# A second ConvGLU's up projection as seven products instead of eight, with the convolution's pad and shift bias moved to ScalarE

## The chip, the core and the metric

The kernel runs on one core of a Trainium2 chip. The time is device microseconds of one execution, the median over runs. TensorE is called PE in the profile, VectorE DVE, ScalarE ACT, GpSimd POOL and SyncE SP.

## The reference

Two layers work on 512 latent and 256 context tokens of width 1024. Layer 0 mixes by windowed attention, layer 1 by a gated recurrence (HGRN2). Each ends with a ConvGLU of width 2816; layer 0 does it for all 768 tokens, layer 1 for the 512 latent ones alone:

```python
def dwconv3(u, w, b):
    up = jnp.pad(u, ((0, 0), (1, 1), (0, 0)))
    return up[:, :-2] * w[0] + up[:, 1:-1] * w[1] + up[:, 2:] * w[2] + b

def conv_glu(h, w_up, conv_w, conv_b, w_down):
    gate, val = jnp.split(h @ w_up, 2, axis=-1)
    return (jax.nn.silu(dwconv3(gate, conv_w, conv_b)) * val) @ w_down
...
        hx2 = rms_norm(x, norm2_g[layer]) * (1.0 + sc2) + sh2
        x = x + g2 * conv_glu(hx2, ffn_w_up[layer], ffn_conv_w[layer], ffn_conv_b[layer], ffn_w_down[layer])
```

Everything is fp32 in and out.

## The kernel before

Activations lie with features on the partitions and tokens along the free axis. An fp32 product is made of three TensorE matmuls in a rounded format: each operand is split into a high part (a rounding copy) and a low part (the remainder), and high by high, high by low and low by high are summed in PSUM.

Weights arrive as fp32 by SP's DMA queue into a raw tile `wr` (pool of two buffers, 1 MB each, two DMAs of 512 KB for one feature tile of the up projection, line 95). ScalarE copies a 512-wide piece into `wh` (L117, or L140 in layer 0's ConvGLU) and VectorE subtracts it to make `wl` (L118, or L141). Pairs `wh`, `wl` come in turn from four pools, some eight pairs ahead of TensorE.

A ConvGLU has 22 feature tiles `ft` of 128 gate and 128 value features. In layer 1 (`ROUNDS[1]`) they go in rounds of 8, 7 and 7 tiles: a round makes its tiles' `g` (the up phase), then the first tile of the next round (`ahead`), and then multiplies the round's tiles into the down projection, eight 128-row blocks of output taken in four pairs (the down phase: matmuls `dn`, accumulated into `xl` by VectorE, L1023). In the last round there is no `ahead`; the first pair's products with all tiles but the last are put before the last tile's `g`. Then come the output's transposes `xo`.

The norm's scale and shift: the matmuls run on activations times gain with the shifts as two extra columns (512 and 513), and the per-token scale `R` is applied to the products as they leave PSUM. `R` is made while tile 0 is multiplied: `nss` sums the squares (L524), VectorE makes `rv` (L428), POOL the inverse root `rs` (L429), VectorE a diagonal `dg` (L529), TensorE spreads it (`nR`, L533), ScalarE copies it to `R`.

Layer 0's ConvGLU uses a scheme that makes the four quadrant products of a 2 by 2 block matrix product with seven products instead of eight. `load_pair` makes four weight totals on VectorE (L136, `s` and two pieces in place in `wr`) and seven operand pairs; `gate_pair` runs the seven products (L188, 84 matmuls of half the columns, PSUM tiles `pZ`, `pY`, `pV`), with ScalarE evacuating four of them, VectorE adding three and multiplying two by `R`, and POOL multiplying the value half by `R`. `combos` makes the seven activation combinations. Layer 1 used `load_w` (four pairs) and `gate_plain` (L912): 96 matmuls of 256 or 258 columns, four multiplies by `R` on VectorE. Both then run the same lines: pad `G` (L983), shift bias `cb` (L985), `u` (ScalarE, L987), two fused multiply-adds (L988, L989), silu (L991), the gate product (L992), and g's high and low parts (L995, L996).

In layer 1 `hgrn_out` runs right ahead: it multiplies the recurrence's output into `xl` in pairs of blocks (L895) and prepares the ConvGLU's activations, so far by `shifts` and `scaled` (L362, L363). The order in which engines get their instructions comes from a scheduler with priorities; weight work is moved ahead by a fixed offset (`W_AHEAD`).

Of the kernel before, what the change touches and what calls it, by code (L numbers as in the profile page):

```python
# [34 lines left out]
SH, C0, TW = 512, 514, 770  # L35
# [29 lines left out]
def ap(t, off, *dims):  # L65
    return bass.AP(t.tensor, t.offset + off, [list(t.ap[0])] + [list(d) for d in dims])
# [6 lines left out]
class Kernel:  # L73
# [442 lines left out]

    def row_factor(self, acc, lat_only, tmp, pp, tag, width, R, sh, dg):


        nc = self.nc  # L520
        nt = (LAT if lat_only else TOK) // P
        ps = pp.tile([P, width], F32, tag=tag, name="nss")
        for i in range(nt):
            nc.tensor.matmul(ps[:, 2 * i:2 * i + 2], lhsT=acc[:, i * P:(i + 1) * P], rhs=self.ones[:, 0:2], start=True, stop=True)  # L524
# [4 lines left out]
        nc.vector.tensor_tensor(dg, ap(self.ident[:, 0:1], 0, (0, nt), (1, P)), ap(r[:, 0:1], 0, (1, nt), (0, P)), op=ALU.mult)  # L529
        for t, c in (((0, 0),) if lat_only else ((0, 0), (4, C0))):  # L530
            m = min(4, nt - t)
            pr = pp.tile([P, width], F32, tag=tag, name="nR")
            nc.tensor.matmul(pr[:, 0:m * P], lhsT=self.ones, rhs=dg[:, t:t + m].rearrange("p t c -> p (t c)"), start=True, stop=True)  # L533
            nc.scalar.activation(R[:, c:c + m * P], pr[:, 0:m * P], AF.Copy)
        nc.vector.memset(R[:, SH:C0], sh)
        if R.shape[1] > TW:
            nc.vector.memset(R[:, TW:], sh)

    def spread(self, r, nt, out, tmp, tag="dg"):

# [354 lines left out]
            self.nc.vector.scalar_tensor_tensor(x[:, d], ps[:, lo:hi], self.modc(l, v, which, d), x[:, d], op0=ALU.mult, op1=ALU.add)  # L895


    def gate_plain(self, ft, ops, hn, G, gg, R, rows, half, tmp, bank):


        nc = self.nc
        act = lambda k: (hn[:, 0, k], hn[:, 1, k])
        cols = ((0, 256), (256, C0))
        for j, dst in enumerate((G[:, 1:1 + C0], gg)):
            ps = [bank("pd")[:, 0:hi - lo] for lo, hi in cols]
            for _ in self.mm_steps(ops[j], range(KT), act, [(o, lo) for o, (lo, _) in zip(ps, cols)]):
                pass
            for _ in rows:
                pass

            for o, (lo, hi) in zip(ps, cols):
                nc.vector.tensor_tensor(dst[:, lo:hi], o, R[:, lo:hi], op=ALU.mult)  # L912
# [45 lines left out]
    def ffn(self, l, hs, R, rows, lat_only, tmp, acp, bk, gp, done, side=None):  # L958
        nc, a = self.nc, self.a
        wup, wdn = a["ffn_w_up"][l], a["ffn_w_down"][l]  # L960
        half = C0 // 2 if lat_only else hs[0].shape[3]
        n = LAT if lat_only else TW
        cw = self.cw[l]

# [8 lines left out]
        def up(ft):  # L973

            ws_ = [self.wcols(wup, ft * P, P), self.wcols(wup, DFF + ft * P, P)]
            ops = self.load_w(ws_) if lat_only else self.load_pair(ws_, tmp)
            if side:
                next(side, None)

            G = tmp.tile([P, 2 * half + 2], F32, tag="G", name="G", bufs=gb)  # L980
            gg = tmp.tile([P, 2 * half], F32, tag="ny", name="gg", bufs=2)
            (self.gate_plain if lat_only else self.gate_pair)(ft, ops, hs, G, gg, R, rows, half, tmp, bank)
            nc.vector.tensor_copy(ap(G[:, 0:1], 0, (TW + 1, nv)), G[:, 1 + SH:1 + SH + nv])  # L983
            cb = tmp.tile([P, 2], F32, tag="cb", name="cb")
            nc.vector.tensor_scalar(cb[:, :nv], G[:, 1 + SH:1 + SH + nv], ws[:, ft:ft + 1], cw[:, 66 + ft:67 + ft], op0=ALU.mult, op1=ALU.add)  # L985
            u = tmp.tile([P, n], F32, tag="nt", name="u", bufs=gb)
            nc.scalar.activation(u, G[:, 1:1 + n], AF.Copy, scale=cw[:, 22 + ft:23 + ft])  # L987
            nc.vector.scalar_tensor_tensor(u, G[:, 0:n], cw[:, ft:ft + 1], u, op0=ALU.mult, op1=ALU.add)  # L988
            nc.vector.scalar_tensor_tensor(u, G[:, 2:2 + n], cw[:, 44 + ft:45 + ft], u, op0=ALU.mult, op1=ALU.add)  # L989
            for v, c, m in segs:  # L990
                nc.scalar.activation(u[:, c:c + m], u[:, c:c + m], AF.Silu, bias=cb[:, v:v + 1])  # L991
                nc.vector.scalar_tensor_tensor(gg[:, c:c + m], gg[:, c:c + m], gg[:, SH + v:SH + v + 1], u[:, c:c + m],  # L992
                                               op0=ALU.subtract, op1=ALU.mult)
            g2 = gp.tile([P, 2, n], F32R, tag="g", name="g")
            nc.scalar.activation(g2[:, 0], gg[:, :n], AF.Copy)  # L995
            nc.vector.tensor_tensor(g2[:, 1], gg[:, :n], f(g2[:, 0]), op=ALU.subtract)  # L996
            return g2
# [273 lines left out]
        es.close()  # L1271
        return part

    def hgrn_out(self, part, hn, acc, tmp, pj):
        nc = self.nc
        self.shifts(1, 1, hn)
        wout = self.a["hgrn_w_out"][0]
        oh = part[0]
        act = lambda k: (oh[:, 0, k], oh[:, 1, k])
        for dp in range(KT // 2):  # L1280
            if dp < 2:
                w, ps, ks = part[1][dp], part[2][dp], (KT - 1,)
# [19 lines left out]
    def run(self, stop=99):  # L1302
# [74 lines left out]
        lv = self.pool(e2, "lv", 2, PSUM)  # L1377
        part = self.hgrn(hn2[0], R, accs[0], hb, pj, lv, sc)
        hc = self.pool(rs, "hC", 1, right=True)
        hn = self.hn_tile(hc, "hn3", C0)  # L1380
        ot = self.pool(es, "ot", 1)
        acc = Rp.tile([P, LAT], F32, tag="acc", name="acc2")
        self.hgrn_out(part, hn, acc, ot, pj)
        if stop == 4:
            self.nc.sync.dma_start(out=self.dbg["dbg"][:, :, :, :LAT], in_=f(part[0][:, :, :, :LAT]))
            e2.close(); rs.close(); es.close(); hB.close(); pjs.close(); top.close(); return
        R = Rp.tile([P, C0], F32, tag="R", name="R2")
        e2.close()
        pjs.close()
        es.close()  # L1390
# [62 lines left out]
```

## Time and profile before

| what | value |
|---|---|
| median of 3 runs | 1862.78 us (1858.02 to 1863.27) |
| the profiled execution | 1863.46 us, span 1861.4 us |
| mean granted TensorE clock | 0.991 |
| layer 1: last part of `hgrn_out` to the end of the row sums | 1439.7 to about 1478 us |
| layer 1, round 0: up from 1481.3, down from | 1581.0 us |
| round 1: up from, down from | 1625.2, 1705.7 us |
| round 2: up from, down from, end of span | 1744.2, 1813.3, 1861.4 us |

Times in the profile's rows are microseconds from the start of the span. A row of stretches gives, for each engine, the busy time and the number of instructions in brackets, then the granted clock as a share of full speed. A row of the timeline gives start, duration, engine, line, operation, the output and inputs, the shape, the count, and in square brackets how long the engine was idle before and what ended that. A row of groups gives the count, busy time and mean duration, and after the second bar the idle time before such instructions with what ended most of it. Instructions of one engine overlap by some tenths of a microsecond, so the distance from start to start is less than a duration.

### The profile page before, as it was taken

Reading aid. Unit: us, or ns where it says so; the run is one execution under the profiler, and the core shown is the slowest. Engines: PE = TensorE matmul, PEld = TensorE weight load, DVE = VectorE, ACT = ScalarE, POOL = GpSimd, SP = SyncE. Lnnn points to the kernel's source line nnn. Section 1 sums busy time; section 2 is a strip of 40 time slices with the busy share of each in tenths; the row PEclk is TensorE's granted clock in tenths of the full one; section 3 lists DMA queues with packets and bytes.
Section 4 is the critical chain, followed back from the end, with each engine's and each line's share of the span. In section 5 each row is a group of like instructions: output and inputs, shape, how many; then the busy total and the mean of one; then the engine's idle time right before and its main releaser. Section 6 shows DMA issues by size and latency. Waiting matters only on the chain.

```text
span 1861.4 us, 32314 instructions
## 1 busy us (share of the span) xinstructions
PE 1798.5 (97%) x13326; PEld 1575.2 (85%) x13326; DVE 1214.4 (65%) x2265; ACT 755.0 (41%) x1486; POOL 218.8 (12%) x219
## 2 busy tenths in 40 slices
PE   6999999998999999999999999999998999999998
PEld 4976786687888888888898888888996799899997
DVE  5576667466868686767777676677765666365462
ACT  4355555465534443434445323333332433233332
POOL 1233333103200000100001100111110000000000
PEclk9999999999999999999999999999999999999999
DMA  9204104232333343333313222121220332333321
GB/s 307 70 23 159 46 24 167 71 102 69 124 114 102 113 136 94 111 96 120 117 54 105 58 58 58 35 56 37 58 69 24 90 92 91 94 96 94 91 83 65
DMA packets 204415, 166.42 MB, mean 89 GB/s; under 512 B 5149, under 2 KB 198254, under 8 KB 199150
## 3 DMA queue, kind: packets, MB, share of 16 engines
q1 hardware_dynamic: 196608, 160.47, 28.1%
q10 hardware_dynamic: 7662, 3.92, 0.7%
q8 instruction: 104, 1.70, 0.4%
q14 instruction: 41, 0.34, 0.1%
HBM read 162.27 MB, written 2.10 MB: 88 GB/s over the span
## 4 chain that ended last, share of the span: by engine, by line
PE 88%; DMA 4%; DVE 4%; ACT 1%; issue 1%; POOL 0%; SPq 0%; ACTq 0%; POOLq 0%; DVEq 0%
PE dn L170 15%; PE pd L170 14%; PE pZ L188 8%; PE pf L170 8%; PE pV L188 4%; PE pjq L598 4%; PE pv L170 4%; PE ao L170 4%; PE ho L170 3%; PE pq L170 3%; PE pv L824 3%; PE pt L816 2%; PE ada L309 2%; PE pgate L170 2%; PE kv L598 2%; DMA wr<-in_ffn_w_up 2%
## 5 line engine op out<-in xcount | busy, mean ns | idle before, releaser
L117 ACT ACTIVATE wh<-wr 128x512 fp32r<-128x512 f32 (+2 forms) x328 | 194.5, 608 | 462.4 <-DMA wr<-in_ffn_w_up 76.9
L118 DVE TENSOR_TENSOR wl<-wr,wh 128x512 fp32r<-128x512 f32 (+2 forms) x328 | 220.0, 678 | 137.6 <-ACT wh L117 137.0
L170 PE MATMUL dn<-g,wh 128*128 128x512 f32 (+1 forms) x1056 | 262.9, 357 | 0.0
L170 PE MATMUL pd<-hn,wh 128*128 128x256 f32 (+1 forms) x1408 | 227.6, 284 | 1.9 <-issue 1.9
L170 PEld LDWEIGHTS dn<-g,wh 128*128 128x128 f32 x1056 | 175.2, 189 | 29.7 <-ACT g L995 0.3
L170 PEld LDWEIGHTS pd<-hn,wh 128*128 128x128 f32 x1408 | 194.5, 190 | 3.3 <-issue 3.1
L188 PE MATMUL pZ<-hs,wh 128*128 128x386 f32 x704 | 184.5, 343 | 2.2 <-DVE hs L393 1.1
L170 PE MATMUL dn<-g,wl 128*128 128x512 f32 (+1 forms) x528 | 159.5, 356 | 0.0
L140 ACT ACTIVATE wh<-wr 128x512 fp32r<-128x512 f32 x132 | 82.3, 629 | 160.5 <-DMA wr<-in_ffn_w_up 38.1
L170 PE MATMUL pd<-hn,wl 128*128 128x256 f32 x704 | 141.9, 283 | 0.0
L188 PEld LDWEIGHTS pZ<-hs,wh 128*128 128x128 f32 x704 | 127.8, 190 | 14.3 <-issue 5.9
L141 DVE TENSOR_TENSOR wl<-wr,wh 128x512 fp32r<-128x512 f32 x132 | 95.9, 733 | 47.9 <-ACT wh L140 46.6
L188 PE MATMUL pZ<-hs,wl 128*128 128x386 f32 x352 | 119.2, 341 | 4.4 <-DVE wl L141 4.4
L170 PE MATMUL pf<-hn,wh 128*128 128x512 f32 (+1 forms) x512 | 117.6, 344 | 2.9 <-DVE xc L1023 1.9
L170 PEld LDWEIGHTS pd<-hn,wl 128*128 128x128 f32 x704 | 109.2, 190 | 0.0
L926 POOL TENSOR_TENSOR gg<-gg,R 128x772 f32<-128x772 f32 x22 | 48.9, 2224 | 456.5 <-DVE gg L925 443.6
L1023 DVE SCALAR_TENSOR_TENSOR xl<-dn,mod,xl 128x512 f32<-128x512 f32 x72 | 53.9, 749 | 73.7 <-PE dn L170 73.7
L170 PEld LDWEIGHTS dn<-g,wl 128*128 128x128 f32 x528 | 87.6, 188 | 14.8
L188 PE MATMUL pV<-hs,wh 128*128 128x386 f32 x352 | 92.0, 340 | 5.0 <-ACT hs L392 5.0
L170 PEld LDWEIGHTS pf<-hn,wh 128*128 128x128 f32 x512 | 79.4, 189 | 15.6 <-DVE xc L1023 2.3
L598 PE MATMUL pjq<-wh,hn 128*128 128x256 f32 x384 | 77.8, 290 | 0.0
L188 PEld LDWEIGHTS pZ<-hs,wl 128*128 128x128 f32 x352 | 66.3, 189 | 7.4 <-DVE wl L141 5.7
(298 smaller groups left out, 3787.0 us busy)
## 6 DMA issues: line engine op xcount, KB each, us to landing
wr<-in_ffn_w_up SPq DMA_DIRECT2D x88, 512.0 KB, 5.2
wada<-in_ada_w SPq DMA_DIRECT2D x40, 1024.0 KB, 4.9
wr<-in_hgrn_w_in SPq DMA_DIRECT2D x40, 512.0 KB, 4.2
ar<-in_ada_w SPq DMA_DIRECT2D x32, 256.0 KB, 7.1
wr<-in_ffn_w_down SPq DMA_DIRECT2D x8, 896.0 KB, 4.8
wr<-in_attn_w_in SPq DMA_DIRECT2D x6, 1024.0 KB, 8.2
wr<-in_ffn_w_down SPq DMA_DIRECT2D x12, 384.0 KB, 3.6
wr<-in_attn_w_out SPq DMA_DIRECT2D x8, 512.0 KB, 5.7
```

The source lines that it names most:

```text
L117: nc.scalar.activation(wh, src, AF.Copy)
L118: nc.vector.tensor_tensor(wl, src, f(wh), op=ALU.subtract)
L140: nc.scalar.activation(ops[i][0], src, AF.Copy)
L141: nc.vector.tensor_tensor(ops[i][1], src, f(ops[i][0]), op=ALU.subtract)
L170: nc.tensor.matmul(o, lhsT=wt, rhs=at[:, t0:t0 + o.shape[1]], start=(first and n == 0 and i == 0), stop=(last and n == len(ks) - 1 and i = ...
L188: self.nc.tensor.matmul(ps, lhsT=wt, rhs=at, start=(first and k == 0 and i == 0), stop=(k == nk - 1 and i == 2), skip_group_check=not first)
L309: nc.tensor.matmul(ps[32 * j:32 * j + 32, 0:512], lhsT=self.cs[:, k, :], rhs=raw[:, j * 512:(j + 1) * 512], start=(k == 0), stop=(k == KT ...
L598: nc.tensor.matmul(out, lhsT=x, rhs=y[:, wk], start=(start and k == 0 and j == 0), stop=(stop and k == KT - 1 and j == 2))
L816: nc.tensor.transpose(pt[:, j * P:(j + 1) * P], pr[j][:, b * P:(b + 1) * P], self.ident)
L824: nc.tensor.matmul(pv[a * HD:(a + 1) * HD, 0:256], lhsT=V[:, tl, g, :], rhs=pT[:, a * 256:(a + 1) * 256], start=(b == 0), stop=(b == len(t ...
L926: times = lambda eng, o, x, y: eng.tensor_tensor(o, x, y, op=ALU.mult)
L1023: nc.vector.scalar_tensor_tensor(x[:, d], o, self.modc(l, v, 5, d), x[:, d], op0=ALU.mult, op1=ALU.add)
```

## The change

Layer 1's up projection goes through `load_pair` and `gate_pair` as layer 0's does, on halves of 258 columns (the first 258 tokens; the other 254 with two shift columns and two zero columns): 84 matmuls of 258 columns for a tile. `hgrn_out` makes the seven activation combinations, the first five for each pair of blocks inside its loop and the last two behind it. POOL's multiply of the value half by `R` then runs in layer 1 too. In both layers the pad and the shift bias become ScalarE instructions. `gate_plain` is gone.

```diff
@@ def spread R @@
-        if R.shape[1] > TW:
-            nc.vector.memset(R[:, TW:], sh)
+        n = C0 if lat_only else TW
+        if R.shape[1] > n:
+            nc.vector.memset(R[:, n:], sh)
...
-    def gate_plain(self, ft, ops, hn, G, gg, R, rows, half, tmp, bank):
...
@@ ffn @@
-        half = C0 // 2 if lat_only else hs[0].shape[3]
+        half = hs[0].shape[3]
...
-            ops = self.load_w(ws_) if lat_only else self.load_pair(ws_, tmp)
+            ops = self.load_pair(ws_, tmp)
...
-            (self.gate_plain if lat_only else self.gate_pair)(ft, ops, hs, G, gg, R, rows, half, tmp, bank)
-            nc.vector.tensor_copy(ap(G[:, 0:1], 0, (TW + 1, nv)), G[:, 1 + SH:1 + SH + nv])
+            self.gate_pair(ft, ops, hs, G, gg, R, rows, half, tmp, bank)
+            nc.scalar.activation(ap(G[:, 0:1], 0, (TW + 1, nv)), G[:, 1 + SH:1 + SH + nv], AF.Copy)
             cb = tmp.tile([P, 2], F32, tag="cb", name="cb")
-            nc.vector.tensor_scalar(cb[:, :nv], G[:, 1 + SH:1 + SH + nv], ws[:, ft:ft + 1], cw[:, 66 + ft:67 + ft], op0=ALU.mult, op1=ALU.add)
+            nc.scalar.activation(cb[:, :nv], G[:, 1 + SH:1 + SH + nv], AF.Identity, scale=ws[:, ft:ft + 1], bias=cw[:, 66 + ft:67 + ft])
...
-    def hgrn_out(self, part, hn, acc, tmp, pj):
+    def hgrn_out(self, part, hs, acc, tmp, pj):
         nc = self.nc
-        self.shifts(1, 1, hn)
+        some = []
...
+            some.append(self.combos(self.halves(1, 1, dp, 258, True, tmp, ("y0", "y1"), 4), dp, hs))
+            next(some[-1])
             for d in (dp, dp + 4):
-                self.scaled(1, 1, d, hn, True)
                 self.square_acc(d, acc, True, tmp, "sg", first=(d == 0))
+        for rest in some:
+            for _ in rest:
+                pass
...
-        hn = self.hn_tile(hc, "hn3", C0)
+        hs1 = hc.tile([P, 7, 2, 4, 258], F32R, tag="hs", name="hs3")
+        hs = [hs1[:, i] for i in range(7)]
...
-        R = Rp.tile([P, C0], F32, tag="R", name="R2")
+        R = Rp.tile([P, 516], F32, tag="R", name="R2")
```

In the changed file the lines of the ConvGLU stand lower: the adds of `gate_pair` are L910, its multiplies L911, pad and bias L968 and L970, the fused operations L973, L974 and L977, the low part of g L981, the residual add of `hgrn_out` L896, and `combos` has L393 (`hs`) and L396 (`y`).

The order of instructions moves as follows. First VectorE between the row sums and the diagonal `dg` that `R` waits for. Before:

```order
L363 SCALAR_TENSOR_TENSOR hn_15134<-xl,gs_126,hn_15134 128x512
L515 TENSOR_TENSOR acc_15138<-acc_15138,sq 128x512
L118 TENSOR_TENSOR wl<-wr,wh 128x512 x2
L428 TENSOR_SCALAR rv<-nss 128x4
L529 TENSOR_TENSOR dg<-cst,rs 128x512
L912 TENSOR_TENSOR G<-pd,R_15337 128x256
```

Changed:

```order
L396 TENSOR_TENSOR y<-y 128x258
L428 TENSOR_SCALAR rv<-nss 128x4
L910 TENSOR_TENSOR G<-t,pY 128x258
L136 TENSOR_TENSOR wr<-wr 128x512
L141 TENSOR_TENSOR wl<-wr,wh 128x512
L396 TENSOR_TENSOR y<-y 128x258 x2
L393 TENSOR_TENSOR hs_15134<-y,hs_15134 128x258
L141 TENSOR_TENSOR wl<-wr,wh 128x512 x3
L393 TENSOR_TENSOR hs_15134<-y,hs_15134 128x258 x2
L529 TENSOR_TENSOR dg<-cst,rs 128x512
```

Eleven instructions, of the last combinations and of the weights of tiles 0 and 1, now stand between `rv` and `dg`, where there was none.

Next VectorE in round 0's up phase, before (most of one tile: two pieces of G, pad and bias, the two fused operations, two pieces of the value, and splits between them):

```order
L912 TENSOR_TENSOR G<-pd,R_15337 128x256
L912 TENSOR_TENSOR G<-pd,R_15337 128x258
L118 TENSOR_TENSOR wl<-wr,wh 128x512
L983 COPY G<-G 128x1
L985 TENSOR_SCALAR cb<-G,wsum,par 128x1
L988 SCALAR_TENSOR_TENSOR u<-G,par,u 128x512
L989 SCALAR_TENSOR_TENSOR u<-G,par,u 128x512
L118 TENSOR_TENSOR wl<-wr,wh 128x512
L912 TENSOR_TENSOR gg<-pd,R_15337 128x256
L912 TENSOR_TENSOR gg<-pd,R_15337 128x258
L118 TENSOR_TENSOR wl<-wr,wh 128x512
L992 SCALAR_TENSOR_TENSOR gg<-gg,u 128x512
```

Changed, from the last split that reads tile 2's raw weights to the first totals of tile 4 (`s_15911` is tile 3's total, `s_16060` tile 4's):

```order
L141 TENSOR_TENSOR wl<-wr,wh 128x512
L910 TENSOR_TENSOR gg<-gg,pV 128x258
L973 SCALAR_TENSOR_TENSOR u<-G,par,u 128x512
L974 SCALAR_TENSOR_TENSOR u<-G,par,u 128x512
L141 TENSOR_TENSOR wl<-wr,wh 128x512
L977 SCALAR_TENSOR_TENSOR gg<-gg,u 128x512
L141 TENSOR_TENSOR wl<-wr,wh 128x512
L910 TENSOR_TENSOR gg<-gg,t 128x258
L136 TENSOR_TENSOR s_16060<-wr 128x512
L910 TENSOR_TENSOR G<-t,pY 128x258
L136 TENSOR_TENSOR wr<-s_15911,wr 128x512
```

The first total of tile 4 needs the raw buffer that this split, the first row, releases, and seven instructions stand between the two.

Last TensorE at the end of the last round's up phase. Before, the last value products are followed by 42 down matmuls in a row and then the first transposes:

```order
L170 MATMUL pd<-hn_15134,wh 128x256
L170 MATMUL pd<-hn_15134,wh 128x258
L170 MATMUL pd<-hn_15134,wl 128x256
L170 MATMUL pd<-hn_15134,wl 128x258
L170 MATMUL dn<-g,wh 128x512 x2
L170 MATMUL dn<-g,wl 128x512
```

Changed, the end of the last product and all that is left before the first transposes:

```order
L188 MATMUL pZ<-hs_15134,wh 128x258 x2
L188 MATMUL pZ<-hs_15134,wl 128x258
L170 MATMUL dn<-g,wh 128x512 x3
L170 MATMUL dn<-g,wl 128x512
L170 MATMUL dn<-g,wh 128x512
L170 MATMUL dn<-g,wl 128x512
L1396 MATMUL xo<-cst,xl 128x128 x4
```

The other 36 down matmuls of that pair now stand among and ahead of the last tile's products. SP's queue has the same loads in the same order, and POOL has 22 multiplies `gg<-gg,R` of 128x516 where it had none.

More of the change, by code (lines that the diff above doesn't have):

```diff
@@ L895, in add_gated @@
             self.nc.vector.scalar_tensor_tensor(x[:, d], ps[:, lo:hi], self.modc(l, v, which, d), x[:, d], op0=ALU.mult, op1=ALU.add)
-    def gate_plain(self, ft, ops, hn, G, gg, R, rows, half, tmp, bank):
[L901 to L912, printed above, removed]
     def gate_pair(self, ft, ops, hs, G, gg, R, rows, half, tmp, bank):
@@ L1379, in run @@
         hc = self.pool(rs, "hC", 1, right=True)
-        hn = self.hn_tile(hc, "hn3", C0)
+        hs1 = hc.tile([P, 7, 2, 4, 258], F32R, tag="hs", name="hs3")
+        hs = [hs1[:, i] for i in range(7)]
         ot = self.pool(es, "ot", 1)
         acc = Rp.tile([P, LAT], F32, tag="acc", name="acc2")
-        self.hgrn_out(part, hn, acc, ot, pj)
+        self.hgrn_out(part, hs, acc, ot, pj)
         if stop == 4:
@@ L1409, in done1 @@
                 nc.sync.dma_start(out=a["out"][0, :, (d - 1) * P:(d + 1) * P].rearrange("(t p) c -> p t c", p=P), in_=ost[0])
-        self.ffn(1, hn, R, rows, True, tmp, acp, bk, gp, done1)
+        self.ffn(1, hs, R, rows, True, tmp, acp, bk, gp, done1)
         es.close()
```

## The prediction

> **What bounds the kernel now.** I read the engine line of the page first, then the chain that ended last, then the last 420 us cut into their stages, since the change lies there.
>
> ```profile
> PE 1798.5 (97%) x13326; PEld 1575.2 (85%) x13326; DVE 1214.4 (65%) x2265; ACT 755.0 (41%) x1486; POOL 218.8 (12%) x219
> ...
> PE 88%; DMA 4%; DVE 4%; ACT 1%; issue 1%; POOL 0%; SPq 0%; ACTq 0%; POOLq 0%; DVEq 0%
> ```
>
> ```profile
> core 0: us, PE busy (x) PEld busy (x) DVE busy (x) ACT busy (x) POOL busy (x), PEclk, DMA share, GB/s
> 520.00:600.00 80.00, 79.58 (x455) 71.68 (x454) 58.28 (x104) 30.23 (x55) 5.95 (x3) 1.00 0.37 116
> 1439.70:1471.40 31.70, 28.47 (x108) 21.64 (x108) 23.40 (x38) 17.02 (x30) 0.00 (x0) 0.88 0.36 100
> 1471.40:1481.30 9.90, 7.32 (x58) 7.03 (x59) 4.31 (x10) 2.51 (x4) 1.01 (x1) 0.99 0.38 106
> 1481.30:1581.00 99.70, 99.70 (x819) 99.18 (x818) 59.30 (x119) 39.88 (x61) 0.00 (x0) 0.98 0.29 85
> 1581.00:1625.20 44.20, 44.20 (x194) 36.10 (x193) 17.43 (x27) 10.44 (x18) 0.00 (x0) 1.00 0.33 96
> 1625.20:1705.70 80.50, 80.50 (x673) 80.48 (x672) 47.32 (x95) 30.23 (x48) 0.00 (x0) 1.00 0.30 88
> 1705.70:1744.20 38.50, 38.50 (x170) 31.53 (x169) 17.04 (x27) 9.89 (x17) 0.00 (x0) 1.00 0.37 107
> 1744.20:1813.30 69.10, 69.10 (x578) 69.06 (x577) 40.29 (x81) 25.40 (x41) 0.00 (x0) 1.00 0.29 86
> 1813.30:1861.40 48.10, 42.94 (x202) 34.61 (x200) 12.44 (x20) 9.98 (x18) 0.00 (x0) 0.99 0.19 63
> ```
>
> TensorE bounds the kernel, and layer 1's ConvGLU most plainly: from 1481.3 to 1813.3 it is never idle. Up phases alternate with down phases (99.7/44.2, 80.5/38.5, 69.1/48.1). In an up phase 672 matmuls take 80.5 us, 0.120 us each; in a down phase 168 take 38.5 us, 0.23 each. A feature tile (96 matmuls) is 11.5 us. VectorE is busy 58 to 59% of the up phases and 39 to 44% of the first two down phases.
>
> **The gain on TensorE.** 84 products in place of 96 per tile: 22 x 12 x 0.120 = 31.7 us over the layer; a tile becomes 84 x 0.120 = 10.1 us. That is the whole gain, and it exists only where the other engines deliver a tile in 10.1 us.
>
> **VectorE per tile.** The prices are start-to-start intervals where it ran without a gap.
>
> ```profile
> 1494.98 0.69 DVE L118 TENSOR_TENSOR wl<-wr,wh 128x512 fp32r<-128x512 f32 x1 [2.43 <-ACT wh L117]
> 1495.59 0.75 DVE L912 TENSOR_TENSOR G<-pd,R 128x256 f32<-128x256 f32 x2
> 1496.26 0.68 DVE L118 TENSOR_TENSOR wl<-wr,wh 128x512 fp32r<-128x512 f32 x1
> 1496.37 0.73 ACT L987 ACTIVATE u<-G,par 128x512 f32<-128x512 f32 x1 [0.90 <-DVE G L912]
> 1496.86 0.15 DVE L983 COPY G<-G 128x1 f32<-128x1 f32 x1
> 1496.92 0.27 DVE L985 TENSOR_SCALAR cb<-G,wsum,par 128x1 f32<-128x1 f32 x1
> 1497.13 0.75 DVE L988 SCALAR_TENSOR_TENSOR u<-G,par,u 128x512 f32<-128x512 f32 x1
> 1497.92 0.75 DVE L989 SCALAR_TENSOR_TENSOR u<-G,par,u 128x512 f32<-128x512 f32 x1
> 1498.59 0.68 DVE L118 TENSOR_TENSOR wl<-wr,wh 128x512 fp32r<-128x512 f32 x1
> 1498.70 0.73 ACT L991 ACTIVATE u<-u,cb 128x512 f32<-128x512 f32 x1 [0.53 <-DVE u L989]
> ...
> 1501.80 0.75 DVE L992 SCALAR_TENSOR_TENSOR gg<-gg,u 128x512 f32<-128x512 f32 x1
> ...
> 1502.58 0.63 ACT L995 ACTIVATE g<-gg 128x512 fp32r<-128x512 f32 x1 [1.54 <-DVE gg L992]
> ```
>
> A 512-wide subtraction costs 0.60 (1496.26 to 1496.86), two 258-wide multiplies 0.67, the fused multiply-add 0.67 (1497.92 to 1498.59), pad and bias together 0.27 (1496.86 to 1497.13). Before: 4 splits 2.4, 4 multiplies 1.3, pad and bias 0.3, three fused 2.0, low half of g 0.6: 6.6 us. After: 4 weight totals and 7 splits 6.6, 5 adds and multiplies 1.7, three fused 2.0, g 0.6: 10.9 us, pad and bias gone to ScalarE. 10.9 is over TensorE's 10.1, so VectorE becomes the longer engine of the up phases. ScalarE goes from 4 to 7 copies (0.6 each at most), adds 4 evacuations and the two small operations, and keeps u, silu and g (2.1): some 8 us, under both; pad and bias lie beside VectorE's weight work, except at the very end.
>
> The gate product gg*R goes to POOL, which has nothing to do in layer 1's up phases today. Layer 0 shows what that does to VectorE:
>
> ```profile
> 660.22 1.84 POOL L926 TENSOR_TENSOR gg<-gg,R 128x772 f32<-128x772 f32 x1 [15.62 <-DVE gg L925]
> 660.43 2.18 DVE L141 TENSOR_TENSOR wl<-wr,wh 128x512 fp32r<-128x512 f32 x1 [0.29 <-ACT wh L140]
> ```
>
> The split that began under POOL's multiply took 2.18 us in place of 0.69 and ended 0.55 after it: VectorE stood still for the rest of it. With 516 columns that is 1.84 x 516/772 = 1.2 us of hold per tile, 0 to 1.2 of it lost. I take 1.0, and half of that again as lying in waits that VectorE has anyway (next term). [...]
>
> **The raw weights' loop.** Two raw buffers: tile k+2's load goes out when VectorE's last split of tile k has read the raw tile, and VectorE's first total needs its second half.
>
> ```profile
> 623.79 0.99 SPq L95 DMA_DIRECT2D wr<-in_ffn_w_up  x2
> ...
> 629.53 0.69 DVE L136 TENSOR_TENSOR s<-wr 128x512 f32<-128x512 f32 x1 [0.33 <-DMA wr<-in_ffn_w_up]
> ```
>
> Issue to use is 5.7 us. In layer 0 other work fills it; in round 0 the new order leaves VectorE only 2.8 to 5.6 us of instructions between the release of tile k and the first total of k+2 (priced as above, for tiles 2 to 8: 2.8, 3.7, 3.9, 5.6, 3.5, 4.4, 4.2), so it idles 3.0, 2.1, 1.9, 0.2, 2.3, 1.4, 1.6: 12.5 us. POOL's multiply falls into three of those gaps. VectorE's pace in round 0 is then 10.9 + 1.3 or so, 12.2 us a tile, slower than today's 11.5.
>
> **The start.** Today the row sums end, and the scale R comes back, with little between:
>
> ```profile
> 1477.32 0.95 PE L524 MATMUL nss<-cst,acc 128*128 128x2 f32 x8
> ...
> 1478.55 0.15 DVE L428 TENSOR_SCALAR rv<-nss 128x4 f32<-128x4 f32 x1
> ...
> 1479.89 0.69 DVE L529 TENSOR_TENSOR dg<-cst,rs 128x512 f32<-128x512 f32 x1 [1.18 <-POOL rs L429]
> ...
> 1480.73 1.59 PE L533 MATMUL nR<-dg,cst 128*128 128x512 f32 x2 [2.46 <-DVE dg L529]
> ```
>
> The activations' seven combinations cost VectorE 11 operations of 0.34 in place of two of 0.67 for each pair of feature blocks, 2.4 us, 9.6 in all, and the last of them, with splits of tiles 0 and 1, stand between rv and dg: 5 us of instructions where today POOL's 1.0 us is all there is. VectorE was idle for 8.3 of the 31.7 us from 1439.7 on, less than the 9.6. Adding VectorE's rows from the last residual add on puts dg's end near 1484.2 (today 1480.6), with only 42 of tile 0's products ahead of nR on TensorE instead of 48. Price: about 4 us (2 to 7).
>
> **Round 0.** From dg VectorE has 80 us of instructions to the last split of tile 8, plus 12.5 us of idling and about 3 of POOL's hold: it ends near 1579.5. TensorE then still has 29 products and 174 down matmuls: 3.5 + 174 x 0.233 = 44 us, so the round ends at 1623.6, against 1625.2 today; if TensorE alone set it, 1486.5 + 714 x 0.120 + 44.8 = 1617. Cross-engine waits of 0.3 us a tile more would make 1626 or 1627. I take nothing gained (+8 to -5).
>
> **Round 1.** VectorE comes out of the down matmuls about 1.7 tiles ahead (17 us of TensorE's work); over the 5.3 tiles left it loses 2.1 us a tile, 11 us. So TensorE sets it: 588 x 0.120 + 168 x 0.233 = 109.8 against 119.0, less 2 us of single stalls: 7.2 gained (3 to 9.2).
>
> **Round 2.** 504 in place of 576 products: 8.6 us, less 2.5 for a first tile that waits on its raw load. Then the tail. Today the last G is evacuated half a tile before the last product, and 42 down matmuls (about 9.8 us) cover the convolution. Now G's second half is the last product of all, and the order runs those down matmuls ahead of it, all but six that need the last g. So this chain lies bare: multiply 0.4, pad 0.3, u 0.7, two fused 1.5, silu 0.7, gate 0.75, g 0.6, from the rows above: 5.2 us with the overlaps. A stall also slows what follows:
>
> ```profile
> 1480.70:1484.30 3.60, 3.57 (x13) 2.81 (x14) 1.10 (x4) 1.11 (x2) 0.00 (x0) 0.57 0.00 0
> ```
>
> After 2.46 us idle the granted clock was 0.57 for 3.6 us: 1.5 us lost. Round 2: 8.6 - 2.5 - 5.2 - 1.5 = -0.6 (-4 to +2).
>
> **Layer 0.** Its pads and biases leave VectorE (0.3 us a tile) for ScalarE (30.23 of 80 us busy). TensorE is busy 79.58 of 80 there, so nothing can be gained; a ScalarE operation of about 0.2 us that now stands in G's chain delays g, which waits for the round's end anyway. Taken as 0 (-3 to +2).
>
> **Sum.** 0 + 7.2 - 0.6 + 0 = 6.6 us, the start being inside round 0. The profiled execution took 1863.46 us, 1861.4 of it span; it becomes 1856.9. It lies 0.7 above the median of the three runs, so the forecast is 1856 us, 0.36% faster. This kernel tells 0.3%, 5.6 us, from no change; the forecast is just past that.
>
> **The rivals.**
> A, the sum above: 1852 to 1860.
> B, VectorE stays hidden: the idling of round 0 vanishes because operands are ready earlier than my addition says. For it: in layer 0 the same scheme holds TensorE at 79.58 of 80. Against it: 455 matmuls took those 79.58 us, so a tile there is 84 x 0.175 = 14.7 us, not 10.1. Round 0 gains 8, round 1 9.2, round 2 1.9: 1844; without the start's and tail's prices it would be 1832.
> C, slower: VectorE's pace in round 0. Each 0.1 us a tile over my 12.2 moves the round's end by 0.9 us, and at 12.9 the gain is gone. Splits wait for ScalarE's copies:
>
> ```profile
> L118 DVE TENSOR_TENSOR wl<-wr,wh 128x512 fp32r<-128x512 f32 x109 | 74.7, 687 | 67.5 <-ACT wh L117 67.4
> ```
>
> That is 0.6 us for each of 109 splits, harmless today since VectorE has time. If 0.25 of it stays at each of seven splits, the pace is 14 us; round 0 ends 16 us later, while rounds 1 and 2 keep most of their gain because TensorE needs 14 us a tile from VectorE there before it stalls: about 1871. Against it: ScalarE is no longer than 8 us a tile, and the waits can coincide with those for the raw load.
> D, POOL's hold falls outside VectorE's other waits, 1.2 us in each of nine tiles instead of 3 in all, with the rest as in A: 1864, between 1860 and 1868. The row at 660.43 speaks for it (VectorE had just come out of a wait for ScalarE there); against it, in round 0's order three of the multiplies come just ahead of a wait for the raw load.
>
> **How the numbers follow.** A 0.45 (half of it below 1857.2, half within), B 0.20 (faster), C 0.20 (slower but for 0.02), D 0.15 (0.10 within, 0.05 slower). Faster 0.44, same 0.33, slower 0.23. The range 1842 to 1872 takes in B's and C's values. A alone has 1852 to 1860.
>
> **What would show it.** Right: TensorE's layer 1 matmuls are 264 fewer at 0.120; VectorE over 85% busy from 1485 to 1580; SP's loads leave about 12 us apart in round 0; TensorE waits there for splits and totals; rounds 1 and 2 closer to 10.1 us a tile; one idle stretch of 5 us just before the last down group; splits of 1.5 us or more under POOL's multiply. Wrong: TensorE over 97% busy through round 0 (B), or rounds 1 and 2 as slow a tile as round 0 (C).

## The result, and the profile after

The changed kernel takes 1874.99 us (four runs, 1873.37 to 1876.83), the one before in the same comparison 1860.97 (1858.02 to 1863.27): ratio 1.0073, 95% interval 1.0061 to 1.0084. It is slower, by about 14 us, and lies 3 us above the top of the forecast's range.

The page of the changed kernel, engines and chain:

```profile
PE 1783.8 (95%) x13062; PEld 1556.0 (83%) x13062; DVE 1319.0 (70%) x2388; ACT 841.3 (45%) x1762; POOL 252.3 (13%) x249
...
PE 79%; DVE 9%; DMA 6%; issue 2%; ACT 2%; POOL 1%; SPq 0%; ACTq 0%; DVEq 0%; POOLq 0%
```

TensorE has its 264 matmuls fewer, but its busy time fell by 14.7 us only, where 264 x 0.120 are 31.7: matmuls at a lowered clock are busy longer (44 of them 7.83 us at a clock of 0.64, 52 of them 6.00 at 1.00, in rows below). Its share of the chain fell from 88 to 79%, and VectorE (4 to 9%) and DMA (4 to 6%) took most of what it lost. The stages of layer 1, in the same columns as before (us, busy time and count of PE, PEld, DVE, ACT, POOL, then the granted clock); the rows are the end of `hgrn_out`, the start up to `nR`, then up and down phases of the three rounds, the last one with the tail:

```profile
1436.50:1464.60 28.10, 28.07 (x108) 21.54 (x108) 24.32 (x52) 19.90 (x50) 0.31 (x8) 0.91 0.27 76
1464.60:1479.50 14.90, 8.17 (x46) 6.97 (x47) 14.78 (x34) 8.47 (x20) 1.02 (x1) 0.76 0.00 0
1479.50:1598.20 118.70, 107.80 (x768) 103.00 (x767) 101.61 (x171) 67.29 (x140) 14.10 (x9) 0.92 0.33 98
1598.20:1632.20 34.00, 34.00 (x149) 27.62 (x148) 21.80 (x33) 10.87 (x19) 0.00 (x0) 1.00 0.34 95
1632.20:1720.20 88.00, 84.47 (x639) 81.54 (x638) 78.48 (x133) 51.62 (x110) 11.89 (x7) 0.98 0.28 84
1720.20:1747.60 27.40, 27.40 (x121) 22.24 (x120) 19.02 (x30) 10.47 (x19) 0.00 (x0) 1.00 0.42 122
1747.60:1823.10 75.50, 72.00 (x541) 69.68 (x539) 63.53 (x110) 43.01 (x92) 10.04 (x6) 0.95 0.28 85
1823.10:1871.60 48.50, 36.60 (x165) 29.14 (x164) 13.00 (x20) 10.93 (x20) 0.00 (x0) 0.93 0.18 63
```

Counted from the last `ho` matmul to the end of round 0, round 1, and round 2 with the tail:

| | start and round 0 | round 1 | round 2 and tail |
|---|---|---|---|
| before | 155.6 us | 119.0 us | 117.2 us |
| changed | 167.6 us | 115.4 us | 124.0 us |
| predicted | 154 us | 111.8 us | 117.8 us |

So 15.2 us are lost in layer 1's ConvGLU, 12 of them before the end of round 0. The last `ho` matmul ended 5.0 us earlier than in the profile of before (1464.57 against 1469.60), 1.8 of which stood before layer 0's ConvGLU; that is why the profiled spans differ by 10.2 us only.

Three things are new in these rows. VectorE is busy 101.6 of 118.7 us in round 0's up phase, where it was 59%. TensorE is idle for 10.9 us in that phase. And the clock of that stretch is 0.92, where it was 0.98. Who made TensorE and VectorE wait from 1480 to 1632 (total, times, longest):

```profile
PE pZ L188 <- ACT wh L140: 4.0, 3, 3.2
PE pV L188 <- DVE wl L141: 2.9, 2, 1.7
PE pZ L188 <- ACT gg L918: 2.4, 1, 2.4
PE pZ L188 <- DVE wl L141: 1.0, 1, 1.0
PE pY L188 <- ACT wh L140: 0.6, 1, 0.6
```

```profile
DVE s L136 <- DMA wr<-in_ffn_w_up: 8.6, 5, 2.6
DVE wl L141 <- ACT wh L140: 8.3, 7, 1.9
DVE gg L977 <- ACT u L976: 3.9, 5, 1.6
```

By what ended them, 7.0 of TensorE's 10.9 us were waits for ScalarE and 3.9 for VectorE. Of VectorE's own waits, 7.4 us for raw loads and only 1.1 for ScalarE's copies fall into the up phase. The longest of TensorE's waits shows how VectorE's lateness arrives at TensorE through ScalarE (timeline, round 0):

```profile
1500.75 0.75 DVE L974 SCALAR_TENSOR_TENSOR u<-G,par,u 128x512 f32<-128x512 f32 x1
...
1501.58 1.28 ACT L976 ACT_TABLE_LOAD   x1 [1.13 <-DVE u L974]
1502.88 0.72 ACT L976 ACTIVATE u<-u,cb 128x512 f32<-128x512 f32 x1
1503.51 0.61 ACT L140 ACTIVATE wh<-wr 128x512 fp32r<-128x512 f32 x1
...
1504.17 0.80 PE L188 MATMUL pZ<-hs,wh 128*128 128x258 f32 x2 [3.17 <-ACT wh L140]
```

ScalarE stood at the silu, waiting 1.1 us for VectorE's `u`, then loaded a table; the weight copy that TensorE needed came only behind it. The table load, 1.28 of the 3.17 us, comes once in layer 1's ConvGLU; the kernel before had it too (1.28 us at 1484.53), and there TensorE did not wait for it. The second longest wait, 2.42 us before 1528.07, came the same way. ScalarE's evacuation into a buffer `gg` stood 1.38 us until VectorE had made the low half of an earlier tile's `g`, and TensorE's next products needed the bank that this evacuation empties:

```profile
1527.63 0.39 ACT L918 ACTIVATE gg<-pZ 128x258 f32<-128x258 f32 x1 [1.38 <-DVE g L981]
```

After its 3.17 us of idling TensorE was slow:

```profile
1504.10:1512.00 7.90, 7.83 (x44) 7.83 (x45) 7.90 (x15) 4.13 (x11) 1.67 (x1) 0.64 0.02 5
1512.00:1518.00 6.00, 6.00 (x52) 6.00 (x52) 5.03 (x9) 3.24 (x8) 1.05 (x1) 1.00 0.61 172
...
1530.00:1538.00 8.00, 8.00 (x55) 8.00 (x55) 6.75 (x14) 3.84 (x8) 1.34 (x1) 0.77 0.11 28
```

With a clock of 0.64 it did 44 matmuls in 7.8 us where the next row has 52 in 6.0: 2.8 us lost on top of the 3.17. The row from 1530.0 is the end of the same after an idle stretch of 2.42. Taken as busy time times the missing share of the clock in 20 us pieces, round 0's up phase lost some 8 us in this way, beside its 10.9 us of idling. Of these, 1.2 us stand in the piece from 1480 to 1500, where the kernel before lost 1.7.

The tail, from the last product's multiply to the down matmuls that wait for the last `g`:

```profile
1823.14 0.43 DVE L911 TENSOR_TENSOR G<-pZ,R 128x258 f32<-128x258 f32 x1 [1.52 <-PE pZ L188]
...
1823.99 0.71 ACT L972 ACTIVATE u<-G,par 128x512 f32<-128x512 f32 x1
...
1824.73 0.75 DVE L973 SCALAR_TENSOR_TENSOR u<-G,par,u 128x512 f32<-128x512 f32 x1 [0.60 <-ACT u L972]
1825.52 0.75 DVE L974 SCALAR_TENSOR_TENSOR u<-G,par,u 128x512 f32<-128x512 f32 x1
1826.37 0.72 ACT L976 ACTIVATE u<-u,cb 128x512 f32<-128x512 f32 x1 [1.67 <-DVE u L974]
1827.19 0.75 DVE L977 SCALAR_TENSOR_TENSOR gg<-gg,u 128x512 f32<-128x512 f32 x1 [0.92 <-ACT u L976]
1828.78 0.63 ACT L117 ACTIVATE wh<-wr 128x512 fp32r<-128x512 f32 x1 [1.69 <-DMA wr<-in_ffn_w_down]
1829.31 0.61 ACT L980 ACTIVATE g<-gg 128x512 fp32r<-128x512 f32 x1
...
1829.98 1.65 PE L170 MATMUL dn<-g,wh 128*128 128x512 f32 x3 [6.87 <-ACT g L980]
```

6.87 us, 1.7 more than the chain of operations alone: the silu's end at 1827.1 and the product's at 1827.9 are about as added up, but ScalarE then stood in front of a weight copy whose raw load came late (the row at 1828.78), and `g` was queued behind it.

### The profile page after: what moved, and what is told of

Its sections match the earlier page's. It is cut to its first block, busy times and chain, and to the rows that moved or that the text cites. A ratio compares the mean times of both kernels' runs of the same rounds, so it can differ in the third digit from the quotient of the medians.

```text
span 1871.6 us, 32302 instructions
## 1 busy us (share of the span) xinstructions
PE 1783.8 (95%) x13062; PEld 1556.0 (83%) x13062; DVE 1319.0 (70%) x2388; ACT 841.3 (45%) x1762; POOL 252.3 (13%) x249
## 3 DMA queue, kind: packets, MB, share of 16 engines
q8 instruction: 102, 1.67, 0.4%
## 4 chain that ended last, share of the span: by engine, by line
PE 79%; DVE 9%; DMA 6%; issue 2%; ACT 2%; POOL 1%; SPq 0%; ACTq 0%; DVEq 0%; POOLq 0%
PE dn L170 15%; PE pZ L188 11%; PE pf L170 8%; PE pV L188 5%; DMA wr<-in_ffn_w_up 4%; PE pjq L599 4%; PE pv L170 4%; PE ao L170 4%; PE ho L170 3%; PE pq L170 3%; PE pv L825 2%; PE pY L188 2%; PE pt L817 2%; DVE wl L141 2%; PE ada L309 2%
## 5 line engine op out<-in xcount | busy, mean ns | idle before, releaser
L188 PE MATMUL pZ<-hs,wh 128*128 128x386 f32 (+1 forms) x1408 | 322.4, 318 | 15.7 <-ACT gg L918 6.9
L140 ACT ACTIVATE wh<-wr 128x512 fp32r<-128x512 f32 x264 | 162.2, 628 | 243.2 <-DVE wr L136 59.1
L188 PEld LDWEIGHTS pZ<-hs,wh 128*128 128x128 f32 x1408 | 242.0, 193 | 31.5 <-issue 10.0
L141 DVE TENSOR_TENSOR wl<-wr,wh 128x512 fp32r<-128x512 f32 x264 | 185.0, 713 | 61.0 <-ACT wh L140 60.4
L188 PE MATMUL pZ<-hs,wl 128*128 128x386 f32 (+1 forms) x704 | 219.6, 315 | 5.0 <-DVE wl L141 5.0
L911 POOL TENSOR_TENSOR gg<-gg,R 128x772 f32<-128x772 f32 (+1 forms) x44 | 82.9, 1884 | 771.1 <-DVE gg L910 723.8
L188 PE MATMUL pV<-hs,wh 128*128 128x386 f32 (+1 forms) x704 | 164.0, 319 | 8.8 <-ACT hs L392 7.5
L188 PEld LDWEIGHTS pV<-hs,wh 128*128 128x128 f32 x704 | 123.0, 196 | 12.9 <-ACT hs L392 8.1
L188 PE MATMUL pV<-hs,wl 128*128 128x386 f32 (+1 forms) x352 | 111.7, 318 | 6.3 <-DVE wl L141 6.3
L188 PE MATMUL pY<-hs,wh 128*128 128x386 f32 (+1 forms) x352 | 82.0, 317 | 1.2 <-ACT wh L140 1.1
```

The lines of the kernel that those rows point to most:

```text
L140: nc.scalar.activation(ops[i][0], src, AF.Copy)
L141: nc.vector.tensor_tensor(ops[i][1], src, f(ops[i][0]), op=ALU.subtract)
L188: self.nc.tensor.matmul(ps, lhsT=wt, rhs=at, start=(first and k == 0 and i == 0), stop=(k == nk - 1 and i == 2), skip_group_check=not first)
L911: times = lambda eng, o, x, y: eng.tensor_tensor(o, x, y, op=ALU.mult)
```

## The experiments

The theory after the result: VectorE's 11.9 us a tile (10.9 of instructions, about 1.0 of POOL's hold), with waits for raw loads on top, make it late in the up phases; TensorE idles in short stretches, directly or behind ScalarE, and some of them cost again through the clock (2.8 us behind the 3.17); the bare tail is a loss by itself. The rivals: POOL's hold, the raw buffers' loop, and pad and bias on ScalarE, each as the one cause. All ratios are to the kernel before, run beside each.

**Without the four totals.** In `load_pair`, for layer 1:

```diff
         def total(o, x, y, op):
+            if lat:
+                return o if o is not s1 else x
             nc.vector.tensor_tensor(o, x, y, op=op)
```

> Leaves out the four weight totals of each layer 1 tile (operands are then raw pieces, so the sums are not the reference's); splits, copies, products and the order of the steps stay. Theory (VectorE's 11.9 us a tile starve TensorE in the up phases, and the idle stretches cost again through the granted clock): VectorE falls to 9.5 us a tile, under TensorE's 10.1; TensorE's idle time in round 0 falls from 10.9 us to under 4, the clock there goes above 0.95, and the time falls by 15 to 22 us, to 1853 to 1860. Rival (the raw buffers' loop and ScalarE's queue set the pace, not VectorE's load): under 5 us gained, over 1870.

Measured: 1851.25 us, ratio 0.9949 (0.9934 to 0.9964). The kernel leaves the totals out, so it computes something else; it measures what 2.4 us of VectorE's time a tile are worth. Without them, 14 us slower turn into 9 to 10 us faster. In the changed kernel TensorE was busy 16.8 and 16.5 us of the two 20 us pieces from 1500 to 1540, at a clock of 0.83; here:

```profile
1500.00:1520.00 20.00, 19.40 (x161) 19.40 (x162) 18.82 (x32) 14.23 (x33) 2.99 (x2) 1.00 0.24 68
1520.00:1540.00 20.00, 19.15 (x157) 18.73 (x156) 18.32 (x31) 14.19 (x31) 2.98 (x2) 1.00 0.38 107
```

Over the whole up phase (1478.5 to 1581.7) TensorE's idle time is 3.5 us and the clock 0.99. VectorE's work on the totals is the lever. The run does not separate their load from their place in the chain: ScalarE's copies, which waited 19.1 us for totals from 1480 to 1632 in the changed kernel, have nothing to wait for there either. The tail is still there (7.0 us idle), as it must be.

**The gate product on VectorE.** In `gate_pair`:

```diff
-        times(nc.gpsimd, gg, gg, R)
+        times(nc.vector if half == 258 else nc.gpsimd, gg, gg, R)
```

> Layer 1's multiply of the value half by R moves from POOL to VectorE. Theory (POOL's hold is one part, about 1.0 us of VectorE's time a tile, the multiply itself costs VectorE 0.6): VectorE gains 0.4 us a tile, 2 to 5 us in all, 1870 to 1873, and no split in layer 1 takes over 1.0 us. Rival (POOL's hold is what made it slower, 1.1 us in each of 22 tiles, doubled by the clock): back to 1860 to 1865.

Measured: 1874.84 us, ratio 1.0072 (1.0057 to 1.0087): no difference. The hold is real: in the changed kernel a total that takes 0.68 us alone (at 1495.04) took 1.45 under POOL's multiply and ended 0.55 after it:

```profile
1505.47 1.67 POOL L911 TENSOR_TENSOR gg<-gg,R 128x516 f32<-128x516 f32 x1 [12.42 <-DVE gg L910]
...
1506.24 1.45 DVE L136 TENSOR_TENSOR wr<-s,wr 128x512 f32<-128x512 f32 x1
```

In the two profiles round 0 (from the last `ho` on) is 4.9 us shorter without the hold and round 1 is 3.8 us longer, so the times agree while the stages do not; why round 1 lost was not taken apart. The 2 to 5 us that the theory expected were not seen in the time, and the rival, that the hold was the cause, fell.

**A third raw buffer in layer 1.** The pools' turns keep the look-ahead at eight operand pairs:

```diff
-        raw = self.wp.tile([P, 2048], F32, tag="wr", name="wr")
+        pool = self.wps[0]
+        self.wps = self.wps[1:] + self.wps[:1]
+        raw = pool.tile([P, 2048], F32, tag="wr", name="wr")
...
-        self.wsp.append(self.pool(es, "wsE", 2))
+        c, dd = [p for p in self.wsp if p is not self.ws0]
+        self.wsp = [self.ws0, c, self.ws0, dd]
+        self.wps = [self.wp, self.pool(es, "wpE", 1), self.wp]
```

> Layer 1 gets a third raw weight buffer; the room comes from one pool of operand pairs, and the turn of the pools is changed so that the look-ahead stays at eight pairs. Theory (waits for the raw loads are a smaller part, 7.4 us in round 0): VectorE's waits for loads vanish, round 0 gains 4 to 7 us and the time is 1866 to 1871; VectorE stays over 90% busy in round 0's up phase. Rival (the raw buffers' loop sets the pace): TensorE's idle time in round 0 goes under 4 us and the time under 1862.

Measured: 1864.06 us, ratio 1.0012 (1.0002 to 1.0021), 11 us less than the changed kernel, 2 us beyond what the theory gave. VectorE's waits for raw loads are gone from round 0's up phase, but TensorE's idle time is 10.9 us as before, and the clock drops as before:

```profile
1520.00:1540.00 20.00, 14.23 (x98) 14.03 (x97) 18.83 (x33) 10.80 (x23) 1.36 (x1) 0.83 0.31 85
```

Start and round 0 take 161.7 us (5.9 less): 68 matmuls in place of 46 ran between the last `ho` and `nR`, and the clock of the up phase is 0.94 in place of 0.92. Round 2 with its tail takes 119.1 (4.9 less: the tail's idle stretch is 4.16 us, since the last down weights are in time and six down matmuls stand behind the last product). The loop was a part, not the pace.

**Pad and bias back to VectorE, seven products kept.**

```diff
-            nc.scalar.activation(ap(G[:, 0:1], 0, (TW + 1, nv)), G[:, 1 + SH:1 + SH + nv], AF.Copy)
+            nc.vector.tensor_copy(ap(G[:, 0:1], 0, (TW + 1, nv)), G[:, 1 + SH:1 + SH + nv])
...
-            nc.scalar.activation(cb[:, :nv], G[:, 1 + SH:1 + SH + nv], AF.Identity, scale=ws[:, ft:ft + 1], bias=cw[:, 66 + ft:67 + ft])
+            nc.vector.tensor_scalar(cb[:, :nv], G[:, 1 + SH:1 + SH + nv], ws[:, ft:ft + 1], cw[:, 66 + ft:67 + ft], op0=ALU.mult, op1=ALU.add)
```

> Pad and shift bias go back to VectorE in both layers; the seven products stay. Theory: 0.3 us more for VectorE in each of 22 layer 1 tiles, half of it seen by TensorE: slower by 2 to 6 us, 1877 to 1881. Rival (pad and bias on ScalarE delay the convolution and hold up ScalarE's weight copies): faster by 4 us or more, under 1871.

Measured: 1879.78 us, ratio 1.0096 (1.0079 to 1.0113), as the theory said. **The pads alone** are the same edit the other way round on the kernel before:

> The kernel before with only the pad and the shift bias on ScalarE, in both layers. Theory (VectorE has time in both layers before the change, so neither its gain nor ScalarE's loss is on the path): 1858 to 1865, no difference. Rival (ScalarE's two small steps delay g and the down phases): 1866 or more.

Measured: 1862.06 us, ratio 0.9985 (0.9976 to 0.9994), a gain of 1 to 4.5 us, too small to be told from no change by this kernel's bound. This part of the change is not what made it slower.

**Only the last tile by eight products.** `gate_eight` multiplies the same activations: the product a11 b11 is copied out and used for both halves, so a tile has 96 matmuls and needs four splits and no totals.

```diff
+            plain = lat_only and ft in PLAIN
+            ops = self.load_w(ws_) if plain else self.load_pair(ws_, tmp)
...
+            prod(a, 0, Z, True)
+            nc.scalar.activation(t, Z, AF.Copy)
+            prod(b, 1, Y, True)
+            nc.vector.tensor_tensor(lo, t, Y, op=ALU.add)
+            prod(a, 2, Z)
+            prod(b, 4, Z)
```

> Only tile 21, the last, goes back to eight products (on the same activations: a11*b11 is kept and used for both halves), gate first and value behind it, so that half a tile of products stands behind the last G. Theory (the tail costs 6.9 us idle and some 2.5 us of lowered clock): the idle stretch before the last down group falls under 2.5 us, TensorE has 12 products more (1.4 us), and the time is 5 to 8 us shorter, 1867 to 1870. Rival (the tail is set by VectorE being late in general, so the stall only moves ahead): under 2 us gained.

Measured: 1871.08 us, ratio 1.0035 (1.0023 to 1.0047), against the changed kernel's 1.0073 some 7 us. Round 2 with its tail takes 114.8 us in place of 124.0; the 6.87 us have become 0.59 and 0.72 in front of the last down matmuls:

```profile
1822.98 0.50 PE L171 MATMUL dn<-g,wh 128*128 128x512 f32 x1 [0.59 <-DVE g L1010]
...
1824.90 1.23 PE L171 MATMUL dn<-g,wh 128*128 128x512 f32 x3 [0.72 <-ACT g L1009]
```

The tail is shown to be a loss of its own.

**Tiles 0, 3, 6 and 21 by eight products** (`PLAIN = (0, 3, 6, 21)`):

> Tiles 0, 3, 6 and 21 of layer 1 by eight products (6.3 us of VectorE instead of 10.9), the other 18 by seven. Theory (VectorE's load in round 0 and the tail): the mean VectorE load of round 0 falls to 10.4 us a tile against TensorE's mean 10.6; TensorE's idle time in round 0 falls from 10.9 us to under 5, the clock there over 0.95, and with the tail as in the run of tile 21 alone the time is 1852 to 1860. Rival (the raw buffers' loop sets round 0, whatever VectorE's load): no more gained than by tile 21 alone, 1866 to 1870.

Measured: 1861.17 us, ratio 0.9981 (0.9968 to 0.9995), 10 us less than with tile 21 alone; 1 us over the expected span, on a chip where the kernel before ran at 1864.74. Start and round 0 take 153.6 us; of the 10.9 us of idling after `nR` 2.5 are left, but 4.9 still stand just before it. TensorE does 36 matmuls more there than with tile 21 alone, and the time is 16 us shorter. The rival (raw loads set round 0 whatever VectorE's load) fell.

**The same four tiles with the third raw buffer:**

> The same four tiles by eight products, and the third raw buffer with it. Theory: VectorE's waits for loads go too, 3 to 6 us less than with the four tiles alone, 1847 to 1856: faster than before. Rival (the third buffer's 11 us came from the tail and the start, which the four tiles mend as well): within 2 us of the four tiles alone.

Measured: 1843.21 us, ratio 0.9885 (0.9871 to 0.9900): 18 us less than the four tiles alone, three times the most that was expected. TensorE from 1520 to 1560:

```profile
1520.00:1540.00 20.00, 20.00 (x168) 19.84 (x167) 20.00 (x34) 12.50 (x28) 3.90 (x2) 1.00 0.48 140
1540.00:1560.00 20.00, 20.00 (x170) 20.00 (x169) 19.94 (x34) 14.08 (x31) 3.00 (x2) 1.00 0.22 72
```

Both engines are full. Start and round 0 take 145.6 us, round 1 114.3, round 2 112.2: all three gained on the run without the buffer (153.6, 117.9, 118.0).

**The third buffer in the kernel before:**

> The kernel before (eight products) with the third raw buffer of the earlier runs and nothing else. Theory (before, TensorE is never idle from 1481 to 1813, so loads wait behind nothing that matters): within 3 us of the kernel before. Rival (the third buffer is a gain of its own, whatever the products): 5 us or more faster, and that much of the four tiles' result is not the change's.

Measured: 1863.14 us, ratio 0.9999 (0.9989 to 1.0009). The buffer was worth nothing here, 11 us with seven products throughout and 18 us with the four tiles; without it VectorE was busy 59, 86 and 83% of round 0's up phase.

**Fewer and more light tiles, with the third buffer.** Tiles 0 and 21:

> Third raw buffer, and only tiles 0 and 21 by eight products: 24 products (2.9 us) fewer than with four tiles, VectorE's load in round 0 higher by 4.6 us in each of tiles 3 and 6. Theory (round 0 needs about a third of its tiles light, since VectorE's 11.9 us a tile are over TensorE's 10.1 also without waits for loads): 3 to 8 us slower than four tiles. Rival (with three buffers VectorE's load no longer matters): 2 to 4 us faster than four tiles.

Tiles 0, 3, 6, 13 and 21:

> Third raw buffer, tiles 0, 3, 6, 13 and 21 by eight products: 12 products (1.4 us) more than with four, VectorE lighter by 4.6 us in round 1, where TensorE stood idle 3.8 us. Theory: within 3 us of four tiles, either way (1.4 us lost against up to 3.8 gained). Rival (round 1 too is held by VectorE throughout): over 3 us faster.

Measured: 1852.53 us, ratio 0.9937 (0.9922 to 0.9951), with two; 1839.91, ratio 0.9874 (0.9859 to 0.9889), with five. Two are 9 to 10 us slower than four, a little more than expected, though TensorE has 24 matmuls fewer: TensorE's idle time in round 0's up phase is 8.4 us against 1.4. Five and four do not differ beyond their intervals. Five tiles is the fastest kernel of the study, 1.1 to 1.4% faster than before.

**Five tiles with the gate product on VectorE:**

> The five tiles and third raw buffer, and layer 1's multiply of the value half by R on VectorE instead of POOL, in all 22 tiles. Theory (POOL's hold takes about 1.0 us of VectorE's time a tile, the multiply itself 0.6; with the seven products alone the move changed nothing because the waits for loads swallowed it): now that those waits are gone, 1 to 4 us faster than the five tiles, and no layer 1 split over 1.0 us. Rival (0.6 us more instructions weigh as much as the hold, part of which falls into idle time): no faster, or up to 3 us slower.

Measured: 1844.69 us, ratio 0.9903 (0.9886 to 0.9919), no faster than with POOL (0.9874) and rather slower; the two intervals just touch. POOL's hold, seen in the totals' mean, is gone, and the multiply stands in VectorE's groups instead. First the run with five tiles, then this one:

```profile
L139 DVE TENSOR_TENSOR wr<-s,wr 128x512 f32<-128x512 f32 x17 | 14.6, 857 | 0.1
```

```profile
L139 DVE TENSOR_TENSOR wr<-s,wr 128x512 f32<-128x512 f32 x17 | 11.7, 690 | 0.1
...
L941 DVE TENSOR_TENSOR gg<-gg,R 128x516 f32<-128x516 f32 x17 | 11.8, 693 | 0.1
```

Of POOL's hold, these totals show 17 x 0.167 = 2.8 us in 22 tiles. Giving 0.6 us of VectorE's time a tile to be rid of it did not pay, so over the 22 tiles the hold costs the path no more than that; my 1.0 of lost time was too high, though single holds are of that size (a total of 1.67 us in place of 0.68, at 1556.35 in the changed kernel). Where the rest of it hides was not taken apart: in each kernel the scheduler also places the steps anew.

## Why the prediction was wrong

The size of the work was right, and its effect on the end was not.

- The gain on TensorE was right in kind: 264 matmuls fewer; the undisturbed rounds with light tiles and the third buffer show it.
- VectorE's pace in round 0 was right. The first totals of tiles 2 and 8 start at 1485.17 and 1558.11: 72.9 us for six tiles, 12.2 us each.

```profile
1485.17 0.69 DVE L136 TENSOR_TENSOR s<-wr 128x512 f32<-128x512 f32 x1 [2.56 <-DMA wr<-in_ffn_w_up]
...
1558.11 0.69 DVE L136 TENSOR_TENSOR s<-wr 128x512 f32<-128x512 f32 x1
...
1578.34 0.69 DVE L141 TENSOR_TENSOR wl<-s,wh 128x512 fp32r<-128x512 f32 x1
```

- The start was right: `nR` comes 15.0 us after the last `ho`, 11.1 before, 3.9 more (4 predicted).
- **The step that failed is round 0's end**: "TensorE then still has 29 products and 174 down matmuls". VectorE's last split of tile 8 ended at 1579.0, against 1574.5 predicted (with the 5 us by which everything stood earlier): 4.5 late. From then on TensorE needed 53.2 us, not 44, and was never idle: it had 72 products left in place of 29, and all 192 of the round's down matmuls. So it was behind by itself, and was not waiting for VectorE's last split. I had taken the later of two engines' ends; but TensorE runs its products in order and waits for single operands, so its idle time adds up (10.9 us) beside VectorE's pace, and the clock adds some 8. I had priced the clock once, for the tail. How much the clock alone cost is read from the rows; no run changed it without changing the idling. Size of this step: 13 us (nR to the round's end 152.7 us, 139.3 predicted).
- Round 1 gained 3.6 us, not 7.2. "2 us of single stalls" were 3.5 us of idling, and the clock of 0.98 on 84.5 us took 1.7 more. That VectorE comes with a lead out of the down phase was right (TensorE was not idle in the round's first 39.8 us), and that the lead holds was not: of the next 25.1 us it was busy 21.7, at a clock of 0.93.
- Round 2 lost 6.8 us, not 0.6: 3.5 idle and a clock of 0.95 on 72 us in the up phase, 7.1 in all, where 2.5 were priced; and the tail 6.87 where the chain gave 5.2, because a late raw load stood in ScalarE's queue ahead of `g`.
- Layer 0 taken as 0: pads alone, in both layers, gave 1 to 4.5 us. In that run's profile the last `ho` ends 1.4 us earlier than before and layer 1's rounds are as long as before, so what it gained stands ahead of layer 1's ConvGLU.
- VectorE's waits for the raw loads of tiles 2 to 8 were 7.4 us, 12.5 predicted; waits for ScalarE's `u` (2.7 us from 1484 to 1580), put at nothing in the forecast, came instead. POOL's multiply, charged 0.5 us a tile of path, is bounded by 0.6 in the runs, taken over the whole layer; in round 0 alone the seven products without the hold were 4.9 us faster.

Of the rivals, C gave a time (1871) near the result, but its mechanism, a pace of 14 us a tile on VectorE, is not what the rows show: the pace was 12.2, VectorE waited 1.1 us in all for copies in the up phase, and TensorE lost the time beside it; that the time came out near is luck. A fell with the step of round 0's end. D, the hold outside VectorE's other waits, gave 1864. Round 0 of the run without the hold, 4.9 us shorter, speaks for some of it there; but that run took 1874.84 us in all, so D is not what made the kernel slower. B did not happen with the seven products alone; TensorE's busy rows in the run with four light tiles and the third buffer are what it described. Of the signs named, VectorE was busy 88% of the time from 1485 to 1580, and SP's loads left some 12 us a tile apart. That ScalarE had room (8 us of 10) was right as a sum, 67.3 of 118.7 us busy, and misled: its queue waits in order for VectorE's convolution (1.13 us ahead of the silu at 1501.58), with weight copies and evacuations behind (the copy at 1503.51, which TensorE had waited 3.17 us for).

## What to carry to other kernels

When a change trades TensorE's work for VectorE's, compare the two engines' times per tile, and where the second comes out longer, do not take the later of their two ends: count every in-order wait on the way, and the slower clock behind it where the rows show one (0.64 behind 3.17 us here). A mixture can be worth more than either pure form: here 17 tiles by the scheme with fewer products and 5 by the one with less VectorE work, with one more raw buffer, beat both by over 1%. A buffer that is worth nothing in one kernel is worth trying again once the balance has moved; and the last tile deserves an order of its own, so that the work that needs no convolution comes last.

## What the runs showed of the hardware

TensorE's clock fell after shorter waits than the tail's 6.87 us. Four of TensorE's stalls in the changed kernel's round 0, and a stretch behind the last two of them:

```profile
1524.18 0.39 PE L188 MATMUL pV<-hs,wl 128*128 128x258 f32 x1 [1.13 <-DVE wl L141]
1528.07 0.80 PE L188 MATMUL pZ<-hs,wh 128*128 128x258 f32 x2 [2.42 <-ACT gg L918]
...
1561.70 0.51 PE L188 MATMUL pY<-hs,wh 128*128 128x258 f32 x2 [0.59 <-ACT wh L140]
1563.20 0.39 PE L188 MATMUL pZ<-hs,wl 128*128 128x258 f32 x1 [0.99 <-DVE wl L141]
```

```profile
1563.00:1572.00 9.00, 8.80 (x61) 8.80 (x62) 8.10 (x15) 4.99 (x12) 0.76 (x1) 0.81 0.35 118
```

After the stall of 1.13 us the next matmuls ran at full pace (two of them in 0.40 us, at 1524.40). The stall of 2.42 us was followed by the slow stretch at 1530 shown above (a clock of 0.77 for 8 us); two of 0.59 and 0.99 us within 2.1 us were followed by 9 us at a mean clock of 0.81, where 61 matmuls ran. Behind 1.75 us, before 1576.28, the clock was 1.00 (30 matmuls in 3.72 us). So the clock fell behind waits of 3.17 us, of 2.42 less than 3 us behind one of 1.13, and of 0.59 and 0.99 close together, and in the kernel before behind one of 2.46 (0.57 for 3.6 us); it did not behind 1.13 or 1.75. What decides between them was not shown.
